# Quarter products in the up-projection, sums of squares ahead of TensorE, and later gate projections in a hybrid decoder layer

## The chip, the core and the metric

The kernel runs on one core of one Trainium2 chip. The metric is device time in microseconds (us). TensorE multiplies matrices into PSUM, VectorE, ScalarE and GpSimd work elementwise, and DMA queues move data; the kernel issues its DMAs from the SP queue. The executions shown for the kernel before took 1553.11, 1553.45 and 1550.46 us, with a median of 1553.11 us.

## What is computed

One inference step of one decoder layer, for 16 learned meta tokens and 1024 prompt tokens and, beside them, 8 samples of 4 tokens each. That makes 1072 columns of 1024 features. Everything is float32.

```
h = rms_norm(x, norm_mix); proj = h @ w_in             # 1024 -> 4104
o_ret = retention(rq, rk, rv) ...                       # 4 heads, chunked, with states
o_gdn = gated delta rule(conv(qkv), gates gb, ga) ...   # 4 heads, chunked, with states
x = x + concat(o_ret * silu(rg), o_gdn * silu(gg)) @ w_out
u = causal width-3 depthwise conv(rms_norm(x, norm_ffn) @ w_up)   # 1024 -> 2 * 2816
gate, val = split(u)
x = x + (silu(gate) * val) @ w_down
y = rms_norm(x, norm_final)
```

The states of retention, of the delta rule and of both convolutions are returned too.

## The kernel before

Activations lie with features on the partitions and tokens along the columns. `ob` holds x and later results; `hh` and `hl` hold the normalised activations as a rounded high part and the remainder. Each weight tile (128 outputs by 1024 inputs) is loaded in two DMAs into `raw`, split into `whi` (a ScalarE cast) and `wlo` (a VectorE subtraction), and a product is three matmuls for each of 8 slices of 128 inputs: high by high, high by low, low by high (`mm3`, line 574). The moving operand is a block of columns.

The order of all instructions is worked out by a planner in the kernel (`Recorder`, lines 206 to 466). Operations are recorded first. Then each engine takes, at the planner's assumed time, the ready operation of the lowest class (`cls`) and the earliest record, given a free buffer in the ring of each tile it needs; buffers of one ring are given out in the order of recording within a stream. Projection matmuls are class 2, most chains class 1, evacuations and weight loads class 0. The result is one fixed order for each engine. All instructions are issued at line 466, so they are told apart by tile names.

The stages:

- Head (lines 634 to 724). x arrives in three blocks of columns, `BLK_A`. For each, `x_sums` squares the eight slices (ScalarE, partly VectorE) and sums each over the features by one-column matmuls against `ones_t`, three for each slice; `x_stats` makes the inverse roots and spreads them over the partitions; `x_split` writes `hh` and `hl`. Eight gate columns (`wg`) are projected block by block in the same loop with `g1` and `g2`, 16 matmuls for each block.
- Mixing (lines 745 to 1228). Gate values first, then jobs in a written order: four delta-rule heads ("g"), four retention heads ("r"), and gate tiles ("w"). Projections in ring `mm` (3 PSUM banks) fill the gaps of the chains, which use ring `mx` (5 banks).
- Output projection (lines 1247 to 1353). Blocks 0 and 1 of `BLK_B` (384, 384 and 290 columns) first, then block 2 with all weights loaded again; the normalisation of finished blocks runs beside it.
- Feed-forward (lines 1355 to 1500). 22 pairs of up tiles, one for the gate and one for the value. `up` (line 1357) makes three blocks of 384, 386 and 292 columns with 24 matmuls each; the convolution is one ScalarE and two VectorE operations for each block; then silu, the product (GpSimd) and a split into `r15`. After each two pairs, a group, `down` (line 1481) adds 8 output tiles by 3 blocks, 6 matmuls each, into `ob`. The down weights are split on GpSimd.
- Tail: in the last group the down tiles go block by block (`final`, line 1396), with the squares, the inverse roots and the scaled output of each block behind it.

Of the kernel before, what the change touches and what calls it, by code (L numbers as in the profile page):

```python
# [45 lines left out]
BLK_B = ((0, 384), (384, 768), (768, 1058))  # L46
# [433 lines left out]
def build(tc, I, O, debug=None):  # L480
# [33 lines left out]
    ring(const, "whi", 2, KD * P, F32R)  # L514
    ring(const, "wlo", 2, KD * P, F32R)
# [48 lines left out]
    def load_w(src, lo_eng=None, tags=("raw", "raw")):  # L564
        with cls(0):
            hi = buf("whi", [P, KD, P])
            lo = buf("wlo", [P, KD, P])
            for a, tag in zip((0, 4), tags):
                raw = buf(tag, [P, 4, P])
                dma(out=raw, in_=src[:, a:a + 4, :])  # L570
                split(hi[:, a:a + 4, :], lo[:, a:a + 4, :], raw, lo_eng or V)
        return hi, lo
# [19 lines left out]
    def fetch(t):  # L592
        if t is not None and t not in wq:
            wq[t] = load_w(w_in[t])
# [13 lines left out]
    def gate_proj(slot, nxt, tag):  # L608
# [7 lines left out]
        proj(gate_tile(slot), nxt, evac)  # L616

    with tc.tile_pool(name="mp", bufs=1) as mp:
# [17 lines left out]
        rsx, ssx, tsx, msx, mhx = (buf("c8", [P, 9]) for _ in range(5))  # L636
        G.memset(ssx, 1.0)
# [8 lines left out]
        def x_sums(i):  # L646
            b0, b1 = BLK_A[i]
            n = b1 - b0
            pss = [bank() for _ in range(3)]
            for k in range(KD):  # L650
                sq = buf(("gkd", "gvb", "gy32")[k % 3], [P, 384])
# [5 lines left out]
                for q in range(3):  # L657
                    c0, c1 = chunk_cols(3 * i + q)
                    T.matmul(pss[q][0:c1 - c0, 0:1], sq[:, c0 - b0:c1 - b0], ones_t[:, 0:1], start=k == 0, stop=k == KD - 1)
            for q in range(3):  # L660
                c = 3 * i + q
                c0, c1 = chunk_cols(c)
                V.tensor_copy(ssx[0:c1 - c0, c:c + 1], pss[q][0:c1 - c0, 0:1])

        def x_stats(i):
            b0, b1 = BLK_A[i]
            cs = slice(3 * i, 3 * i + 3)
            ss, ms, mh, rs_, t_ = (b[:, cs] for b in (ssx, msx, mhx, rsx, tsx))
            V.tensor_scalar(out=ms, in0=ss, scalar1=1.0 / D, scalar2=EPS, op0=ALU.mult, op1=ALU.add)
# [27 lines left out]
        g1 = buf("whi", [P, KD, P])  # L697
        g2 = buf("wlo", [P, KD, P])
        graw = buf("c40", [P, KD, 8])
        dma(out=graw, in_=I["wg"])  # L700
        fetch(16)
        x_cols(1, 4)
        x_cols(2, 4)
        last = R.ops[-1]
        for g in (g1, g2):
# [5 lines left out]
        for i, (b0, b1) in enumerate(BLK_A):  # L711
            x_split(i, spread)
            if i < 2:
                spread, last_sqrt = x_stats(i + 1)
# [849 lines left out]
```

## Time and profile before

| | us |
|---|---|
| median of the runs shown | 1553.11 |
| the profiled execution | 1549.05 |
| its span, first to last instruction | 1547.2 |
| TensorE busy | 1505.8 |
| VectorE busy | 976.2 |
| ScalarE busy | 582.3 |
| GpSimd busy | 301.3 |

The profile shows one execution. Busy times on TensorE overlap, because matmuls are pipelined and a row's own length reaches past the next row's start; what a matmul costs is read from the distance of two starts. "Idle before" names the work that released an engine. Times of stretches count from the span's start.

### The profile page before, as it was taken

The page shows a single profiled execution, that of the slowest core. Times are in us where ns is not written, and L with a number is a line of the kernel's source. Part 1 is how long each engine was busy: PE and PEld are TensorE (multiplying, and loading weights), DVE is VectorE, ACT ScalarE, POOL GpSimd, SP SyncE. Part 2 cuts the span into 40 slices and gives each one's busy share as a digit, 9 for nine tenths or more (in the row PEclk, how much of TensorE's full clock was granted, in tenths as well). Part 3 has the DMA queues.
Part 4 walks back from the last instruction along what each step waited for, and adds up shares of the span by engine and source line. Part 5 has one row for each costly group of instructions (what it writes and reads, how often), then busy time and mean ns, then how long its engine had stood idle before and what let it go on. Part 6 is the DMA issues. An engine that isn't in the chain of part 4 may idle for free.

```text
span 1547.2 us, 25949 instructions
## 1 busy us (share of the span) xinstructions
PE 1505.8 (97%) x9875; PEld 1453.0 (94%) x9875; DVE 976.2 (63%) x2411; ACT 582.3 (38%) x1553; POOL 301.3 (19%) x365
## 2 busy tenths in 40 slices
PE   7999999999999999999999999999999999999994
PEld 7898988999899899999999999999999999999994
DVE  4787787787768856647854545545554545555547
ACT  4553453455346335424532232324132231324123
POOL 1221202202120221501320212113020212112022
PEclk9999999999999999999999999999999999999997
DMA  5121202111120211523120110202021111202103
GB/s 189 30 72 29 84 20 70 43 59 60 41 81 28 63 33 53 183 83 96 49 76 28 56 60 25 75 23 70 20 64 28 56 52 33 68 29 70 42 1 114
DMA packets 63689, 91.06 MB, mean 59 GB/s; under 512 B 13060, under 2 KB 31948, under 8 KB 63436
## 3 DMA queue, kind: packets, MB, share of 16 engines
q1 hardware_dynamic: 63564, 89.40, 18.3%
q8 instruction: 78, 1.28, 0.4%
q14 instruction: 47, 0.39, 0.1%
HBM read 79.71 MB, written 9.66 MB: 58 GB/s over the span
## 4 chain that ended last, share of the span: by engine, by line
PE 90%; DVE 6%; DMA 1%; issue 1%; ACT 1%; POOL 0%; SPq 0%; DVEq 0%; ACTq 0%; POOLq 0%
PE mm L466 61%; PE mx L466 29%; DVE wlo L466 1%; DVE ob L466 1%; DMA ob<-in_xt 1%; DVE sw L466 1%; DVE c L466 1%; DMA gbq<-scr_rows 0%; ACT f2k L466 0%; SPq L466 0%; POOL f2k L466 0%; DVE f2k L466 0%; DVE t2k L466 0%; DVE gvb L466 0%; DVE hl L466 0%
## 5 line engine op out<-in xcount | busy, mean ns | idle before, releaser
L466 PE MATMUL mm<-hh,whi 128*128 128x384 f32 (+5 forms) x1952 | 643.5, 330 | 1.7 <-ACT hh L466 1.0
L466 PE MATMUL mm<-hh,wlo 128*128 128x384 f32 (+5 forms) x1952 | 644.5, 330 | 0.0
L466 PE MATMUL mm<-hl,whi 128*128 128x384 f32 (+5 forms) x1952 | 642.3, 329 | 0.4 <-POOL hl L466 0.3
L466 PEld LDWEIGHTS mm<-hh,whi 128*128 128x128 f32 x1952 | 368.8, 189 | 4.8 <-issue 1.5
L466 PEld LDWEIGHTS mm<-hl,whi 128*128 128x128 f32 x1952 | 369.2, 189 | 3.2 <-issue 0.9
L466 PEld LDWEIGHTS mm<-hh,wlo 128*128 128x128 f32 x1952 | 368.6, 189 | 1.7 <-issue 0.5
L466 DVE SCALAR_TENSOR_TENSOR f2k<-mm,wc,f2k 128x352 f32<-128x352 f32 (+2 forms) x264 | 150.9, 572 | 160.7 <-ACT f2k L466 80.0
L466 PE MATMUL mx<-r,dhl 128*128 128x384 f32 (+1 forms) x1440 | 232.5, 321 | 0.0
L466 PEld LDWEIGHTS mx<-r,dhl 128*128 128x128 f32 x1440 | 231.9, 188 | 0.0
L466 ACT ACTIVATE f2k<-mm,wc 128x352 f32<-128x352 f32 (+1 forms) x132 | 72.0, 545 | 306.7 <-PE mm L466 306.7
L466 DVE TENSOR_TENSOR ob<-mx,ob 128x384 f32<-128x384 f32 (+1 forms) x240 | 123.3, 524 | 100.7 <-PE mx L466 98.4
L466 DVE TENSOR_TENSOR wlo<-raw,whi 128x512 fp32r<-128x512 f32 x170 | 137.2, 820 | 33.1 <-ACT whi L466 32.6
L466 ACT CAST whi<-raw 128x512 fp32r<-128x512 f32 x170 | 103.9, 620 | 43.5 <-PE mm L466 36.0
L466 POOL TENSOR_TENSOR f2k<-f2k,f2k 128x384 f32<-128x384 f32 (+1 forms) x75 | 76.6, 1022 | 173.4 <-DVE f2k L466 160.1
L466 POOL TENSOR_SCALAR f2k<-su,wc 128x32 f32<-128x32 f32 x44 | 13.5, 306 | 443.9 <-ACT su L466 443.9
L466 POOL TENSOR_TENSOR ob<-ob,sw 128x384 f32<-128x384 f32 (+1 forms) x39 | 41.9, 1074 | 210.5 <-DVE sw L466 145.4
L466 ACT ACTIVATE f2k<-f2k 128x384 f32<-128x384 f32 (+1 forms) x66 | 32.9, 499 | 115.8 <-DVE f2k L466 115.8
L466 DVE TENSOR_TENSOR r<-f2k,r 128x384 fp32r<-128x384 f32 (+1 forms) x66 | 34.8, 528 | 60.3 <-ACT r L466 60.2
L466 ACT CAST r<-f2k 128x384 fp32r<-128x384 f32 (+1 forms) x66 | 32.4, 490 | 93.7 <-POOL f2k L466 93.7
L466 POOL TENSOR_TENSOR dhl<-f2k,dhl 128x512 fp32r<-128x512 f32 x44 | 55.6, 1298 | 11.8 <-ACT dhl L466 11.8
L466 DVE SCALAR_TENSOR_TENSOR ob<-mm,wc,ob 128x384 f32<-128x384 f32 (+3 forms) x90 | 51.3, 570 | 1.7 <-ACT ob L466 1.2
L466 DVE TENSOR_TENSOR ob<-mm,ob 128x384 f32<-128x384 f32 (+1 forms) x48 | 25.0, 522 | 38.4 <-PE mm L466 38.1
(282 smaller groups left out, 1830.7 us busy)
## 6 DMA issues: line engine op xcount, KB each, us to landing
raw<-in_w_up SPq DMA_DIRECT2D x88, 256.0 KB, 2.7
raw<-in_w_in SPq DMA_DIRECT2D x64, 256.0 KB, 2.9
f2k<-in_w_down SPq DMA_DIRECT2D x44, 256.0 KB, 4.5
raw<-in_w_out SPq DMA_DIRECT2D x18, 256.0 KB, 2.8
gbq<-scr_rows SPq DMA_DIRECT2D x16, 256.0 KB, 4.2
out<-sst SPq DMA_DIRECT2D x8, 512.0 KB, 2.6
wr<-in_w_out SPq DMA_DIRECT2D x14, 256.0 KB, 3.0
ob<-in_xt SPq DMA_DIRECT2D x4, 768.0 KB, 8.3
```

Of the source, the lines that this page charges most:

```text
L466: f(*a, **k)
```

## The change

Head: the squares of eight slices are added elementwise into two accumulators, and only these are summed over the features, by six one-column matmuls a block. The gate projection and its chain move into a function `gates`, recorded behind the second delta-rule tile, and use ring `mm`. The low parts of three early weight tiles (16, 20, 24) are made on GpSimd. Weight buffers are rings of half tiles.

Output projection: blocks are 508, 276 and 274 columns wide, with the two narrow ones first and the wide one last; three weight tiles are kept for both rounds. While the wide block is projected, the narrow ones are normalised and the operand sums of the quarter products are formed (`norm_others`); the wide one is normalised inside the first pair (`norm_first`).

Feed-forward: for the two narrow blocks, a pair of up tiles (two row blocks), the two halves of the inputs and the two blocks of columns make a 2 by 2 product of quarters, computed with seven products instead of eight, from sums of weights (on GpSimd) and sums of activations, and additions of results (on VectorE). The wide block is projected as before. The down-projection takes two banks of `mx` as ring `dn`, and its weights come in quarters.

```diff
-BLK_B = ((0, 384), (384, 768), (768, 1058))
+BLK_O = ((0, 508), (508, 784), (784, 1058))
+BLK_B = ((0, 510), (510, 784), (784, 1058))
+WS = 276
+HB = (508, 782)
...
-    ring(const, "whi", 2, KD * P, F32R)
-    ring(const, "wlo", 2, KD * P, F32R)
+    ring(const, "whi", 4, KD * P // 2, F32R)
+    ring(const, "wlo", 4, KD * P // 2, F32R)
...
-            wq[t] = load_w(w_in[t])
+            wq[t] = load_w(w_in[t], G if t in (16, 20, 24) else None)
...
-            pss = [bank() for _ in range(3)]
+            acc = []
             for k in range(KD):
...
-                for q in range(3):
-                    c0, c1 = chunk_cols(3 * i + q)
-                    T.matmul(pss[q][0:c1 - c0, 0:1], sq[:, c0 - b0:c1 - b0], ones_t[:, 0:1], start=k == 0, stop=k == KD - 1)
+                if k < 2:
+                    acc.append(sq)
+                else:
+                    (V if k % 2 else G).tensor_tensor(out=acc[k % 2][:, 0:n], in0=acc[k % 2][:, 0:n], in1=sq[:, 0:n], op=ALU.add)
+            pss = bank()
...
+                for j in range(2):
+                    op = T.matmul(pss[0:c1 - c0, q:q + 1], acc[j][:, c0 - b0:c1 - b0], ones_t[:, 0:1], start=j == 0, stop=j == 1)
...
-        dma(out=graw, in_=I["wg"])
         fetch(16)
         x_cols(1, 4)
+        dma(out=graw, in_=I["wg"])
...
+                if h == 0 and i == 1:
+                    R.stream = 3
+                    gates()
+                    R.stream = 0
...
+        for tag, n, e, dt in (("al", 4, 512, F32R), ("as", 8, 274, F32R), ("dhl", 4, 512, F32R), ("f2k", 5, 512, F32), ("ds", 8, WS, F32),
+                              ("rawd", 1, 512, F32), ("su", 6, NB * 6, F32), ("uo", 2, 72, F32), ("c3", 8, 4, F32)):
...
+        R.rings["dn"] = Ring(mx.bufs)
+        mx.free.sort(key=lambda f: f[1])
+        R.rings["dn"].free = [mx.free.pop() for _ in range(2)]
+        more("raw", 2, F32)
+        more("whi", 2, F32R)
+        more("wlo", 2, F32R)
...
-        gate_proj(3, None, "f2k")
+        gate_proj(3, None, "f2k", BLK_A[::-1])
...
+        def prod(out, a, x, first=True, last=True):
+            with cls(2):
+                for k in range(4):
+                    xh, xl = x(k)
+                    T.matmul(out, a[0][:, k, :], xh, start=first and k == 0, stop=False)
+                    T.matmul(out, a[0][:, k, :], xl, start=False, stop=False)
+                    T.matmul(out, a[1][:, k, :], xh, start=False, stop=last and k == 3)
...
+                r11, r12, r21, r22 = (load_half(w_up[f], a) for f in fs for a in (0, 4))
+                a11, a12, a21, a22 = (unit(r) for r in (r11, r12, r21, r22))
+                G.tensor_tensor(out=r22, in0=r21, in1=r22, op=ALU.add)
+                G.tensor_tensor(out=r21, in0=r11, in1=r21, op=ALU.subtract)
+                G.tensor_tensor(out=r11, in0=r22, in1=r11, op=ALU.subtract)
+                G.tensor_tensor(out=r12, in0=r12, in1=r11, op=ALU.subtract)
+                s2, s1 = (unit(r) for r in (r11, r22))
+                s3, s4 = (unit(r, None, ("al", "al") if late else ("whi", "wlo")) for r in (r21, r12))
...
+            x = one(a11, B11)
+            m1 = buf("ds", [P, WS])
+            with cls(0):
+                S.copy(m1, x)
+            g1 = []
+            if late is None:
+                first_block(lambda: g1.append(second()))
+            else:
+                g1.append(second())
+            v = one(a22, T4, "mx")
+            u2 = buf("ds", [P, WS])
+            add(u2, one(s2, T2), m1)
+            z = one(s1, T1)
+            u3 = buf("ds", [P, WS])
+            add(u3, one(s3, T3), u2)
+            add(u2, z, u2)
+            v1_ = conv(add(v, v, u3), NF + p, 1, uo, None)
+            v2_ = conv(add(z, z, u3), NF + p, 2, uo, None)
+            z = one(s4, B22)
+            g2_ = conv(add(z, z, u2), p, 2, uo, None)
+            if late is not None:
+                late()
+                first_block()
...
+            R.stream = 1
             if not tail:
...
+                wd = [down_weights(mq) for mq in range(2)]
+                for m in range(4):
+                    down(wd[m // 2], m, 0)
+                for m in range(4):
+                    for t in (1, 2):
+                        down(wd[m // 2], m, t)
+                for mq in (2, 3):
+                    wd = down_weights(mq)
+                    for m in (2 * mq, 2 * mq + 1):
                         for t in range(3):
-                            down(wd, m, t, "mx")
+                            down(wd, m, t)
...
```

Here `first_block` projects the wide block for both tiles of the pair (24 matmuls each in ring `mx`), `second` is the product of `a12` with `B21`, added to `m1`, and `conv` is the convolution. The lines above leave out the new bodies of `norm_others`, `norm_first`, `gates` and `down_weights`, whose work the text above tells.

## Rows read from the trace of the kernel before

**Rows 1.** The page's part 1: busy time of each engine, share of the span.
```profile
PE 1505.8 (97%) x9875; PEld 1453.0 (94%) x9875; DVE 976.2 (63%) x2411; ACT 582.3 (38%) x1553; POOL 301.3 (19%) x365
```
**Rows 2.** The chain that ended last, one feed-forward group: start, us, what.
```profile
1101.53 46.86 PE mm L466 x288
1148.40 23.09 PE mx L466 x144
```
**Rows 3.** Busy times by stretch: length, PE, PEld, DVE, ACT, POOL, granted clock, DMA.
```profile
62.00:630.00 568.00, 557.40 (x4081) 512.54 (x4080) 433.55 (x1302) 269.46 (x816) 110.31 (x138) 1.00 0.17 53
720.00:770.00 50.00, 47.67 (x313) 45.76 (x312) 45.40 (x107) 26.23 (x59) 15.51 (x18) 1.00 0.21 66
837.00:907.00 70.00, 70.00 (x434) 70.00 (x434) 36.61 (x70) 20.05 (x49) 12.32 (x14) 1.00 0.15 47
1510.20:1530.00 19.80, 12.98 (x73) 12.17 (x72) 14.67 (x35) 11.89 (x29) 9.60 (x11) 0.74 0.07 23
```
**Rows 4.** Timeline of TensorE in the feed-forward: start, us, engine, instruction.
```profile
894.52 0.30 PE L466 MATMUL mm<-hh,whi 128*128 128x292 f32 x1
...
897.78 0.34 PE L466 MATMUL mm<-hh,whi 128*128 128x384 f32 x1
...
901.97 0.34 PE L466 MATMUL mm<-hh,whi 128*128 128x386 f32 x1
```
**Rows 5.** Instruction groups, 837 to 907 us: count, busy, mean ns, idle before.
```profile
L466 DVE TENSOR_TENSOR wlo<-raw,whi 128x512 fp32r<-128x512 f32 x8 | 6.9, 861 | 2.8 <-ACT whi L466 2.8
L466 POOL TENSOR_TENSOR dhl<-f2k,dhl 128x512 fp32r<-128x512 f32 x4 | 5.1, 1300 | 1.1 <-ACT dhl L466 1.1
L466 ACT CAST whi<-raw 128x512 fp32r<-128x512 f32 x8 | 5.0, 622 | 1.9 <-PE mm L466 1.9
...
L466 DVE TENSOR_TENSOR ob<-mx,ob 128x290 f32<-128x290 f32 x8 | 3.7, 459 | 1.5 <-PE mx L466 1.4
```
**Rows 6.** Timeline of TensorE in the head, 0 to 62 us.
```profile
4.54 1.23 PE L466 MATMUL mx<-ones_t,gkd 128*48 128x1 f32 x6 [4.54 <-ACT gkd L466]
...
12.82 1.26 PE L466 MATMUL mx<-ones_t,gvb 128*48 128x1 f32 x6
...
23.78 0.60 PE L466 MATMUL mm<-hh,whi 128*128 128x304 f32 x1
...
31.83 0.46 PE L466 MATMUL mm<-hh,wlo 128*128 128x304 f32 x1
32.08 0.46 PE L466 MATMUL mm<-hh,whi 128*128 128x304 f32 x1
...
33.62 0.30 PE L466 MATMUL mm<-hl,whi 128*128 128x304 f32 x1
33.77 0.30 PE L466 MATMUL mm<-hh,wlo 128*128 128x304 f32 x1
...
46.18 0.53 PE L466 MATMUL mm<-hh,whi 128*128 128x388 f32 x1
```
**Rows 7.** Timeline of VectorE in the head, 0 to 62 us.
```profile
20.32 1.42 DVE L466 SCALAR_TENSOR_TENSOR t2k<-ob,wc,mx 128x304 f32<-128x304 f32 x3 [2.14 <-PE mx L466]
```
**Rows 8.** The chain that ended last, 740 to 770 us.
```profile
752.96 0.75 PE mx L466 x6
...
762.10 0.81 POOL hl L466
```
**Rows 9.** Timeline of all engines in the tail, 1503 to 1548 us.
```profile
1510.68 6.72 ACT L466 ACTIVATE f2k<-ob 128x384 f32<-128x384 f32 x16
...
1512.05 8.24 POOL L466 TENSOR_TENSOR f2k<-f2k,f2k 128x290 f32<-128x290 f32 x7 [19.18 <-DVE f2k L466]
...
1521.20 4.79 PE L466 MATMUL mm<-r,dhl 128*128 128x290 f32 x22 [0.82 <-DVE r L466]
...
1538.75 5.13 DVE L466 SCALAR_TENSOR_TENSOR ob<-ob,wc,mx 128x384 f32<-128x384 f32 x11
```
**Rows 10.** One tile's view, wlo, 780 to 1500 us: durations ns min/median/max, starts.
```profile
L466 DVE TENSOR_TENSOR wlo<-raw,whi x80: 691/693/1368, 781.2 to 1470.4; 128x512 fp32r<-128x512 f32 x80
```

More of the change, by code (lines that the diff above doesn't have):

```diff
@@ L1225, in build @@
         wq[None] = wo[0]
-        keep = [v.vt for t in wq.values() for v in t]
+        keep = [v.vt for t in wq.values() for x in t for v in x.parts]
         for v in keep:
@@ new lines, in sums, with up_pair, one, add @@
+        def sums(i):
+            return lambda k: (th[:, i, k, :], tl[:, i, k, :])
+        B11, B21 = (cols(k, slice(HB[0], HB[0] + WS)) for k in (0, 4))
+        B22, T1 = cols(4, slice(HB[1], HB[1] + WS)), cols(0, slice(BLK_O[2][0], BLK_O[2][0] + WS))
+        T2, T3, T4 = (sums(i) for i in range(3))
+        def up_pair(p, uo, late=None):
+            fs = (p, NF + p)
+            sus = []
+            with cls(0):
+                for f in fs:
+                    su = buf("su", [P, NB, 6])
+                    dma(out=su, in_=I["sff"][:, f * NB * 6:(f + 1) * NB * 6].rearrange("p (b t) -> p b t", b=NB))
+                    sus.append(su)
+                r11, r12, r21, r22 = (load_half(w_up[f], a) for f in fs for a in (0, 4))
[6 more added lines that the diff above has]
+                s3, s4 = (unit(r, None, ("al", "al") if late else ("whi", "wlo")) for r in (r21, r12))
+            def one(a, b, tag="mm"):
+                out = bank(tag)[:, 0:WS]
+                prod(out, a, b)
+                return out
+            def add(out, a, b):
+                with cls(0):
+                    V.tensor_tensor(out=out, in0=a, in1=b, op=ALU.add)
+                return out
+            whole = []
+            def first_block(then=None):
+                for f, (ka, kb) in zip(fs, ((a11, a12), (a21, a22))):
+                    out = bank()[:, 0:510]
+                    prod(out, ka, cols(0, CL), last=False)
+                    prod(out, kb, cols(4, CL), first=False)
+                    whole.append(conv(out, f, 0, uo, sus[f // NF]))
+                    if then is not None and f == p:
+                        then()
+            def second():
+                x2 = one(a12, B21)
+                return conv(add(x2, x2, m1), p, 1, uo, None)
+            x = one(a11, B11)
+            m1 = buf("ds", [P, WS])
+            with cls(0):
+                S.copy(m1, x)
[18 more added lines that the diff above has]
+                first_block()
+            return (whole[0], g1[0], g2_), (whole[1], v1_, v2_)
@@ L1430, in final @@
                 rb = bank()
[L1431 removed]
+                dg = buf("f2k", [P, 4, P])
                 for i, (a, b) in enumerate(cuts):
```

445 lines of the change are left out of this document (238 added, 207 removed).

## Prediction

> **What bounds the kernel now.** I read the page's busy times first. TensorE is busy 97% of the span, VectorE 63%, ScalarE 38%, GpSimd 19% [rows 1]: the matmuls are the candidate. Busy time on TensorE is not proof, so I read the chain of waits next. In the feed-forward it is nothing but matmuls: 46.86 us for 288 up-projection matmuls, 23.09 us for 144 down-projection ones [rows 2]. That pair of rows repeats, one pair of lines for each of the 11 groups (the last is drawn out by the tail). One group takes 69.95 us and TensorE idles in none of it, while VectorE is busy 36.61 of 70 us, ScalarE 20.05, GpSimd 12.32 [rows 3]. So half of the execution (770 us) is bound by the number and width of matmuls alone, and only fewer columns can shorten it.
>
> The stretch views show three places of another kind. In the mixing stretch (62 to 630 us) VectorE is 76% busy and TensorE idles 10.6 of 568 us, 1.9% [rows 3]. At the junction of output projection and feed-forward (720 to 770 us) VectorE is 91% busy, and TensorE idles 2.3 of 50 us [rows 3]. In the head and in the tail TensorE waits for chains; both are priced below.
>
> **The feed-forward.** For each pair of 128-row up tiles the old code runs 2 x 3 blocks x 24 matmuls of 384, 386 and 292 columns. The new one runs 2 x 24 matmuls of 510 columns and seven products of 12 matmuls of 276 columns, where eight would be needed in the plain way. What does a matmul of each width cost? I take start-to-start times, since TensorE is pipelined and a row's own length is not its price. 24 starts of 292 columns, 894.52 to 897.78 us, give 0.1358 us each; the next 24 of 384 columns, to 901.97, give 0.1746 [rows 4]. The line through the two is 0.00042 us per column. It gives 0.129 us for 276 columns and 0.228 for 510; neither width occurs in the trace. Bounds: 276 columns lie between 0.128 (in proportion to 292) and 0.136 (no faster than 292, if the weight load sets a floor there); 510 lie between 0.226 and 0.232 (in proportion to 384). I take the line, because 276 is only 16 columns from a measured width.
>
> A group holds two pairs. Its up part becomes 96 x 0.228 + 168 x 0.129 = 21.9 + 21.7 = 43.6 us, against 46.86: 3.3 us less, 36 us over 11 groups. The bounds: 96 x 0.226 + 168 x 0.128 = 43.2 (40 us gained) and 96 x 0.232 + 168 x 0.136 = 45.1 (19 us gained). The down part keeps its 144 matmuls, now of 510, 274 and 274 columns: 48 x (0.228 + 2 x 0.128) = 23.2 us instead of 23.09, 1 us lost in all. The output projection changes its widths in the same way, 192 x (0.227 + 0.129 + 0.128) us, under 1 us of difference.
>
> The Trainium skill speaks of this sum: "TensorE: Matmul & The Clock Gate", section "Back-to-back issue gap", puts an isolated full-clock matmul at its columns over 2.4 GHz plus 2.5 ns. That would be 162.5 ns for 384 columns, where rows 4 have 174.6. By it the up part would go from 43.2 us to 40.4 and the gain would be 31 us: the same sign, a little less. The rows decide.
>
> **What the seven products cost the other engines.** For each pair, eight half-size weight units are split into high and low parts instead of four: four more ScalarE casts of 0.622 us and four more VectorE subtractions of 0.861 us [rows 5]. Four 512-column sums of weights go to GpSimd, priced by its 512-column subtraction of 1.300 us. Seven additions from PSUM go to VectorE, by the 290-column addition of 0.459 us [rows 5]. For each group of two pairs that is, on VectorE, 8 x 0.861 + 14 x 0.459 = 13.3 us more, 36.6 to 49.9; ScalarE goes from 20.1 to about 26.8 (two copies of some 0.4 us with it), GpSimd from 12.3 to 22.7. All three still fit under the 66.8 us of TensorE. But VectorE would be 75% busy, and TensorE has less room to wait: two of the five mx banks become a ring of their own for the down tiles ("dn"), a product must wait for its bank, and a bank is held until VectorE has added and convolved. Queued behind a late addition on VectorE are the convolution taps, then the gate product, then the split that the down matmuls read. These waits do not occur in the trace of before; I bound them by two stretches. At 53% of VectorE TensorE waits for nothing (lower end 0). At 76% it idles 1.9%, which is 1.25 us of a group. At 91%, at the junction, it idles 4.7%, 3.1 us of a group (upper end, 34 us in all). The load of 75% is nearest to the mixing stretch, so I take 1.25 us x 11 = 14 us. The added DMA issues (44 small loads of conv states in place of one) go to the SP queue, which issues in a fraction of a microsecond; they stand ahead of weights that are asked for a pair in advance, so I price them at nothing; uncovered, the weights would come late once a pair and this would be part of the 14 us.
>
> **Head.** TensorE starts the one-column sums of block 0 at 4.54 us and the last run until about 14 us; VectorE begins to normalise block 0 only at 20.32 us [rows 6, 7]. TensorE then alternates projections with the one-column sums of blocks 1 and 2, and the 24 matmuls of the first projection block, begun at 23.78, are followed by the next block only at 46.18 [rows 6]. Moreover it runs at the 1.2 GHz level there: 304 columns start 0.25 us apart at 31.8 and 0.15 apart at 33.6 [rows 6]. The change removes 54 of 72 one-column matmuls and adds 18 elementwise additions on VectorE and GpSimd. Block 0's sums then end some 4 us earlier, because six matmuls follow the last square instead of a queue of 24 fed since 4.54. The gates' 48 matmuls are moved, not removed; behind two tiles they run at full clock. Their chain of small operations on ScalarE, VectorE and GpSimd must then be done before the first recurrent job, with one more tile as cover (24 x 0.15 + 48 x 0.175 = 12 us); if that falls short, other projections fill in. Their weight load moves behind block 1's input on the SP queue and is needed only two tiles later: nothing. What is late next is the split of blocks 1 and 2 on VectorE, which also does the convolutions there. Lower end of the gain: 3 us, the earlier first split less one addition of about 1 us. Upper end: 13 us, the 54 matmuls at about 0.2 us (11 us) and the first tile at full speed. I take 8. It passes to the end, since TensorE has projections left to fill with when mixing ends.
>
> **Junction.** The last output tiles now belong to the widest block, and its normalisation is hidden behind pair 0's seven products, 84 x 0.129 = 10.8 us. Before, the chain from the sums at 752.96 us to the last awaited split, ending at 762.91 [rows 8], is 10 us for 290 columns. With 508 columns each of its long operations is 1.6 times as long, so some 14 to 17 us; the 5.5 us of the first wide product use the split rows one by one. I expect the same loss as before, 0, within 4 us either way.
>
> **Tail.** ScalarE's squares (6.72 us from 1510.68) and GpSimd's additions (8.24 us from 1512.05) stand ahead of the last block's gate product and split, so its down matmuls run in earnest only from 1521.20 [rows 9]. Between 1510.2 and 1530 TensorE is busy 12.98 of 19.8 us, at a mean granted clock of 0.74 [rows 3]. In the new order the wide block's 48 down matmuls (10.9 us) and the middle block's (6.2 us) lie behind the last product: 17 us of work cover an 11 us chain. Then the end is VectorE's: its last scalings run to 1543.9 [rows 9], and their columns stay the same. Gain from 0 (VectorE bound all through) to 12 (the idle 6.8 us and the slow clock); I take 8.
>
> **The sum** is made against the profiled execution, 1549.05 us with a span of 1547.2: -36 + 2 (other widths) + 14 (waits) - 8 - 8 = -36. The median of the runs shown, 1553.11, is 4 us above that execution, so the forecast on the scale of the runs is 1517 us.
>
> **Rivals.** (a) The planner hides all waits: 0 instead of 14, head and tail at 11 each: -36 + 2 - 22 = -56, 1497 us. For it: the old feed-forward has not one wait. Against it: VectorE had 47% free there. (b) The waits are those of the junction, 34 us, and tail and head give 4 each: -36 + 2 + 34 - 8 = -8, 1545 us. For it: two down banks, and additions, taps and weight splits falling together in a pair's second half.
> (c) Slower: GpSimd's added work blocks VectorE until VectorE is the bound. In the feed-forward the weight subtraction takes 0.691 to 1.368 us with a median of 0.693 [rows 10]: some take twice as long. If the added GpSimd operations doubled all 16 weight subtractions and the 6 of the activations, VectorE would need 49.9 + 16 x (1.368 - 0.861) + 6 x 0.5 = 61 us a group; adding a doubling of the 24 down additions that fall to it (by 0.5) gives 73 us. From 71.4 us a group (69.95 plus the head's and the tail's 16 us over 11) the kernel is slower; at 73, 11 x 3 - 16 = +18, 1571 us. Against it: GpSimd has work for only a third of a group, and the down additions read one operand from PSUM.
> The Trainium skill has the rule behind this rival: "SBUF — State Buffer", section "Who interferes with whom", says that a VectorE instruction with two SBUF inputs contends with a GpSimd one that reads SBUF, and that the loser waits for the whole instruction. The maximum in rows 10 agrees; that PSUM additions should be free of it speaks against (c).
> (d) The seven products do not shorten TensorE because 276 columns meet a floor: at 0.136 us the feed-forward gains 19 instead of 36; it is in the bounds, 1534 us.
>
> **Chances.** Forecast, 1502 to 1535 us with the floor of (d) at its upper end: 0.50. (a): 0.22. (b): 0.14. Within 0.2%, about what a measurement of this kernel can tell from no change (1550 to 1556): 0.04. (c): 0.10. So faster 0.86, same 0.04, slower 0.10. The range takes in (a) and most of (b): 1493 to 1545.
>
> **What would show it.** Steps: 84 products a pair about 0.129 us apart and 48 about 0.228; the chain's up pieces near 43.6 us a group; VectorE near 50 us a group. Wrong if: idle time of TensorE before "mm" or "dn" matmuls released by VectorE exceeds 3 us a group; VectorE is over 90% busy there; the first split is not before 17 us; TensorE still idles over 5 us after the last product.

## The result, and the profile after

The changed kernel takes 1531.89 us (median of 4 runs, 1531.76 to 1533.05) beside 1552.3 us of the kernel before on the same chip: a ratio of 0.9871, interval 0.9854 to 0.9888. That is 20 us less; the profiled spans, 1547.2 and 1530.1 us, give 17.1. The forecast was 36 us less. The sign holds and the time lies in the range; half of the gain is missing, so the question is where it went. Line 466 of before is line 469 here.

Busy times after, part 1 of the page (before: rows 1), and busy times by stretch (columns as in rows 3):
```profile
PE 1471.4 (96%) x9513; PEld 1329.2 (87%) x9513; DVE 1127.7 (74%) x2661; ACT 643.9 (42%) x1684; POOL 459.6 (30%) x502
...
62.00:630.00 568.00, 561.36 (x4082) 511.48 (x4081) 428.48 (x1300) 268.72 (x811) 110.31 (x140) 1.00 0.17 52
720.00:770.00 50.00, 42.80 (x215) 37.16 (x215) 42.07 (x78) 23.82 (x54) 28.15 (x25) 0.93 0.17 53
837.00:904.40 67.40, 67.30 (x409) 60.60 (x408) 49.20 (x92) 25.14 (x58) 23.20 (x22) 1.00 0.16 50
645.00:657.00 12.00, 7.39 (x37) 6.73 (x37) 10.04 (x20) 8.78 (x32) 12.00 (x22) 0.72 0.60 178
```
The feed-forward group (third stretch) is close to the forecast: 67.4 us instead of 69.95, with VectorE busy 49.2, ScalarE 25.1 and GpSimd 23.2 us (forecast: 66.8 and 1.25 of waits, 49.9, 26.8 and 22.7). The junction (second) is not: TensorE idles 7.2 of 50 us, where it was 2.3 [rows 3], and the mean granted clock is 0.93. The last stretch, the start of the output projection, is new: TensorE is busy 7.4 of 12 us at a clock of 0.72. In the kernel before, the same stretch is full:
```profile
645.00:657.00 12.00, 12.00 (x71) 12.00 (x70) 10.58 (x14) 6.33 (x15) 7.94 (x8) 1.00 0.98 313
```

The starts of TensorE at the borders of the parts (first matmul of the output projection, first of the feed-forward, last of the last product), in the kernel before and in the changed one:
```profile
645.02 0.52 PE L466 MATMUL mm<-r,whi 128*128 128x384 f32 x2
...
741.44 0.34 PE L466 MATMUL mm<-hh,whi 128*128 128x384 f32 x1
...
1509.91 0.30 PE L466 MATMUL mm<-hh,wlo 128*128 128x292 f32 x1
```
```profile
643.22 0.36 PE L469 MATMUL mm<-th,whi 128*128 128x276 f32 x1 [0.49 <-POOL tl L469]
...
748.56 0.29 PE L469 MATMUL mm<-hh,whi 128*128 128x276 f32 x1
...
1484.50 0.29 PE L469 MATMUL mm<-hh,wlo 128*128 128x276 f32 x1
```
From these starts the difference of the two profiled executions splits up like this (us):

| part | forecast | measured |
|---|---|---|
| up to the first matmul of the output projection (645.02, now 643.22) | -8 | -1.8 |
| output projection (96.4, now 105.3) | under +1 | +8.9 |
| first pair of the feed-forward (junction) | 0 | +10.3 |
| 11 groups (69.95, now 67.41 each) | -36 + 1 + 14 = -21 | -27.9 |
| tail (time behind the last product less its down matmuls: 31.6, now 24.9) | -8 | -6.7 |
| sum | -36 | -17.2 (17.1 by the rounded spans) |

The junction's line is what is left of the stretch from output projection to last product (768.6, now 736.1) after the groups' 27.9 us and 14.9 us of down matmuls that have moved behind the last product. There are 36 of 510 and 96 of 274 columns there now, 20.5 us at 0.232 and 0.127 us each; there were 42 of 290 columns, 5.6 us at 0.133. The measured column compares one execution of each kernel. In the eight profiles below and above that have the changed head, the last projection matmul starts between 640.4 and 642.7 us, so the first line is known to about 2 us.

TensorE in one group after, and the same matmul eight groups later (timeline; answers rows 4):
```profile
848.82 0.29 PE L469 MATMUL mm<-hh,whi 128*128 128x276 f32 x1
...
851.87 0.63 PE L469 MATMUL mx<-al,dhl 128*128 128x510 f32 x2
...
856.34 0.39 PE L469 MATMUL mx<-hh,whix 128*128 128x510 f32 x1
...
861.91 0.29 PE L469 MATMUL mm<-hh,whix 128*128 128x276 f32 x1
...
1388.09 0.29 PE L469 MATMUL mm<-hh,whi 128*128 128x276 f32 x1
```
24 starts of 276 columns, 848.82 to 851.87, are 0.127 us each; 24 of 510, 856.34 to 861.91, are 0.232. The forecast had 0.129 and 0.228. (1388.09 - 848.82) / 8 = 67.41 us a group.

TensorE's waits at the two places that cost 19 us (timeline; in brackets the idle time and what ended it):
```profile
650.10 0.60 PE L469 MATMUL mm<-th,whi 128*128 128x276 f32 x1 [3.60 <-ACT th L469]
651.68 0.60 PE L469 MATMUL mm<-tl,whi 128*128 128x276 f32 x1 [0.98 <-DVE tl L469]
...
753.10 0.29 PE L469 MATMUL mx<-th,whix 128*128 128x276 f32 x1
759.35 1.85 PE L469 MATMUL mx<-ones_t,f2k 128*128 128x1 f32 x8 [5.96 <-DVE f2k L469]
```
At 753 us one matmul of a product is followed by the wide block's sums of squares, and TensorE's queue stands for 6 us. What it waits for, on ScalarE, GpSimd and VectorE:
```profile
755.76 0.62 ACT L469 CAST al<-raw 128x512 fp32r<-128x512 f32 x1 [3.76 <-POOL raw L469]
756.29 0.62 ACT L469 ACTIVATE f2k<-ob 128x508 f32<-128x508 f32 x1
...
753.26 1.25 POOL L469 TENSOR_TENSOR f2k<-f2k,f2k 128x508 f32<-128x508 f32 x1
754.47 1.26 POOL L469 TENSOR_TENSOR raw<-rawx,raw 128x512 f32<-128x512 f32 x1
...
757.15 1.59 POOL L469 TENSOR_TENSOR rawx<-rawx,rawx 128x512 f32<-128x512 f32 x1
...
756.41 1.21 DVE L469 TENSOR_TENSOR al<-raw,al 128x512 fp32r<-128x512 f32 x1 [3.87 <-ACT al L469]
757.54 1.75 DVE L469 TENSOR_TENSOR f2k<-f2k,f2k 128x508 f32<-128x508 f32 x1
```
The last square (ScalarE, 756.29) is queued behind a cast that waits for GpSimd's sums of weights, and the last sum of squares (VectorE, 757.54) behind the subtraction that follows that cast. And it takes 1.75 us for 508 columns.

The head (timelines of VectorE, GpSimd, TensorE):
```profile
17.07 0.97 DVE L469 SCALAR_TENSOR_TENSOR t2k<-ob,wc,mx 128x304 f32<-128x304 f32 x2 [0.89 <-PE mx L469]
...
32.20 3.44 DVE L469 SCALAR_TENSOR_TENSOR ob<-sc,wc,ob 128x32 f32<-128x32 f32 x3
...
32.13 1.30 POOL L469 TENSOR_TENSOR wlo<-raw,whi 128x512 fp32r<-128x512 f32 x1 [0.21 <-ACT whi L469]
33.39 0.99 POOL L469 TENSOR_TENSOR gkd<-gkd,gy 128x384 f32<-128x384 f32 x1
34.34 1.26 POOL L469 TENSOR_TENSOR wlo<-raw,whi 128x512 fp32r<-128x512 f32 x1
...
36.77 0.44 PE L469 MATMUL mm<-hh,whi 128*128 128x388 f32 x1 [3.66 <-ACT hh L469]
```
The first split comes at 17.07 instead of 20.32 us [rows 7], 3.25 us earlier, near the 3 us forecast. But then three VectorE operations of 32 columns take 3.44 us, and TensorE waits 3.66 us for the split queued behind them.

### The profile page after: what moved, and what is told of

Its sections match the earlier page's. It is cut to its first block, busy times and chain, and to the rows that moved or that the text cites. A ratio compares the mean times of both kernels' runs of the same rounds, so it can differ in the third digit from the quotient of the medians.

```text
span 1530.1 us, 25981 instructions
## 1 busy us (share of the span) xinstructions
PE 1471.4 (96%) x9513; PEld 1329.2 (87%) x9513; DVE 1127.7 (74%) x2661; ACT 643.9 (42%) x1684; POOL 459.6 (30%) x502
## 4 chain that ended last, share of the span: by engine, by line
PE 84%; DVE 11%; ACT 2%; issue 2%; DMA 1%; POOL 0%; SPq 0%; DVEq 0%; ACTq 0%; POOLq 0%
PE mx L469 45%; PE mm L469 39%; DVE ob L469 2%; DVE wlo L469 2%; DVE ds L469 1%; DVE c L469 1%; DVE hl L469 1%; DVE f2k L469 1%; DVE sw L469 1%; DVE t2k L469 0%; DVE wlox L469 0%; DMA ob<-in_xt 0%; DVE gvb L469 0%; ACT jk L469 0%; ACT hh L469 0%
## 5 line engine op out<-in xcount | busy, mean ns | idle before, releaser
L469 PE MATMUL mm<-hh,whi 128*128 128x384 f32 (+5 forms) x1084 | 357.7, 330 | 6.7 <-ACT hh L469 5.5
L469 PE MATMUL mm<-hl,whi 128*128 128x384 f32 (+5 forms) x1084 | 357.5, 330 | 2.9 <-DVE hl L469 2.9
L469 PE MATMUL mm<-hh,wlo 128*128 128x384 f32 (+5 forms) x1084 | 357.4, 330 | 0.0
L469 PEld LDWEIGHTS mm<-hh,whi 128*128 128x128 f32 x1084 | 206.6, 191 | 13.9 <-ACT hh L469 6.5
L469 PEld LDWEIGHTS mm<-hl,whi 128*128 128x128 f32 x1084 | 206.6, 191 | 9.9 <-DVE hl L469 4.2
L469 PEld LDWEIGHTS mm<-hh,wlo 128*128 128x128 f32 x1084 | 206.7, 191 | 4.3 <-issue 1.3
L469 DVE TENSOR_TENSOR ob<-mx,ob 128x274 f32<-128x274 f32 (+1 forms) x264 | 136.0, 522 | 99.5 <-PE mx L469 96.4
L469 PEld LDWEIGHTS mx<-as,dhl 128*128 128x128 f32 x1008 | 143.2, 190 | 16.7 <-DVE ob L469 8.5
L469 PE MATMUL mx<-as,dhl 128*128 128x274 f32 x1008 | 153.3, 293 | 1.4 <-DVE ob L469 0.4
L469 PE MATMUL mx<-al,dhl 128*128 128x510 f32 x504 | 134.2, 394 | 3.1 <-ACT al L469 2.0
```

Source lines behind the costliest of these rows:

```text
L469: f(*a, **k)
```

## Experiments

The changed kernel was timed once more beside the first three (1533.5 us; ratio 0.9881, 0.9866 to 0.9895, span 1531.7). Differences below are from that run.

**What do the seven products give?** Eight plain products in the same new order:
```diff
-            v = one(a22, T4, "mx")
...
-            g2_ = conv(add(z, z, u2), p, 2, uo, None)
+            v1_ = conv(two(a21, a22, B11, B21, "mx"), NF + p, 1, uo, None)
+            v2_ = conv(two(a21, a22, B12, B22), NF + p, 2, uo, None)
+            g2_ = conv(two(a11, a12, B12, B22), p, 2, uo, None)
```


> The changed kernel with the plain eight quarter products (96 matmuls of 276 columns a pair instead of 84), with no sums of weights, no sums of inputs and no additions from PSUM, in the same order of blocks and with the same head and tail. Theory 1 (the feed-forward is bound by the columns that TensorE streams, 0.127 us a matmul of 276, and the elementwise work of the seven products hides): a group of the feed-forward takes 24 x 0.127 = 3.0 us more than the changed kernel's 67.4, so 70.4, that is 33 us over 11 groups; less up to 5 us at the junction, where the sums of inputs and weights are gone: 28 to 34 us slower than the changed kernel, ratio to the kernel before 1.005 to 1.010. Rival (the seven products pay a good part of their saving back in waits, as the forecast had it with 1.25 us a group): a group takes 1.5 to 2.3 us more than 67.4 and the whole is 12 to 24 us slower than the changed kernel.

1545.67 us, ratio 0.997 (0.9959 to 0.9982), span 12.1 us longer. The whole is in the rival's range, the group between the two. TensorE's timeline of this run, one matmul eight groups apart, and its stretches:
```profile
832.82 0.29 PE L469 MATMUL mx<-hh,whi 128*128 128x276 f32 x1
...
1391.54 0.29 PE L469 MATMUL mx<-hh,whi 128*128 128x276 f32 x1
...
720.00:770.00 50.00, 50.00 (x270) 43.41 (x269) 37.04 (x77) 25.58 (x52) 19.46 (x17) 1.00 0.24 71
```
A group takes 69.84 us, 2.43 more than 67.41; the columns alone would make 24 x 0.127 = 3.05. So the seven products give back 0.6 us a group. Eleven groups would make 27 us, but the whole is only 12 longer: outside the steady groups the plain products save some 15 us. Split as in the table above, 9 of these lie at the junction, 3 in the tail and the rest ahead of the feed-forward, where profiles of the same work differ by 1 to 2 us. At the junction TensorE is busy 50.00 of 50 us at the full clock. The junction's loss thus belongs to the seven products, whose first pair needs sums of inputs and of weights all at once, and not to the new order of the blocks.

**Is the junction's wait one of order?** Wide tiles' evacuation first, combined weights of pair 0 behind it:
```diff
+            with cls(-1 if w > 2 * KD - 4 else R.cls):
...
-                (G if KD < w < 2 * KD - 1 else V).tensor_tensor(out=acc[:, 0:n], in0=acc[:, 0:n], in1=sq[:, 0:n], op=ALU.add)
+                    done[0] = (G if KD < w < 2 * KD - 2 else V).tensor_tensor(out=acc[:, 0:n], in0=acc[:, 0:n], in1=sq[:, 0:n], op=ALU.add)
...
+                    for op in R.ops[n0:]:
+                        if op.eng == "S":
+                            op.preds.add(done[0])
```


> The changed kernel with another order at the junction: additions, squares and sums of the last three wide output tiles go ahead of weight work on every engine, the last two sums of squares are on VectorE instead of GpSimd, and the casts of pair 0's four combined weight units stand behind the last sum. Theory 1 (TensorE's 6.25 us wait at 753 us is one of order: the last sum of squares is queued on GpSimd and VectorE behind sums and splits of weights): the wait falls under 2.5 us and the whole is 4 to 8 us shorter than the changed kernel. Rival (VectorE has too much to do there, as it was 91% busy at the junction before): the wait only moves to the wide block's splits or to the combined weights, and the whole is within 1.5 us of the changed kernel.

1525.84 us, ratio 0.9838 (0.9825 to 0.9852): 7.7 us shorter by the medians, 6.7 by the ratios, theory 1. From the first feed-forward matmul to the last product it takes 731.5 us instead of 736.1. The wait of TensorE falls from 6.0 to 3.55 us, not under 2.5. What is left of it shows on VectorE and GpSimd in this run:
```profile
754.86 1.72 DVE L469 TENSOR_TENSOR f2k<-f2k,f2k 128x508 f32<-128x508 f32 x1 [0.69 <-ACT f2k L469]
...
754.78 1.26 POOL L469 TENSOR_TENSOR rawx<-raw,rawx 128x512 f32<-128x512 f32 x1
756.12 1.60 POOL L469 TENSOR_TENSOR rawx<-rawx,rawx 128x512 f32<-128x512 f32 x1
```
The last sum of squares still takes 1.72 us while GpSimd adds weights. With pair 0's sums of weights on VectorE (the run of both places, below) the same operation takes
```profile
753.40 0.69 DVE L469 TENSOR_TENSOR f2k<-f2k,f2k 128x508 f32<-128x508 f32 x1 [0.69 <-ACT f2k L469]
```

**The start of the output projection.**
```diff
             def down_weights(mq, tags=("dhl", "dhl")):
-                with cls(0):
+                with cls(0 if gp else 1):
```


> The changed kernel with the first group's down-projection weights asked for and split in program order instead of as early as possible, so that their ScalarE casts and GpSimd subtractions no longer stand among the evacuations of the last gate tile. Theory 1 (the two waits of 3.9 and 1.6 us at 646 to 652 us, and the clock of 0.5 that follows them, come from these casts and subtractions): waits together under 2.5 us and the whole 3 to 8 us shorter. Rival (the chain tanh, product, gate product, cast, subtraction is that long by itself behind the last gate block): the waits stay above 4 us and the whole is within 1.5 us of the changed kernel.

1529.69 us, ratio 0.9861 (0.9848 to 0.9875): 3 to 4 us shorter, with an interval that overlaps the changed kernel's. The time alone does not settle it; the first wait does, which is 3.6 us in every profile that leaves this place as it was and 2.22 here. With the second, 1.58, the waits are 3.8 us together: between the two theories. The casts and subtractions of the down weights were part of the cause. The rest, as far as this run's rows show it, is the last gate tile's own chain and a weight subtraction of 1.52 us on VectorE in the middle of it.

**Does VectorE's share make the waits?** The four sums of weights of each pair on VectorE:
```diff
-                G.tensor_tensor(out=r22, in0=r21, in1=r22, op=ALU.add)
+                V.tensor_tensor(out=r22, in0=r21, in1=r22, op=ALU.add)
...
```


> The changed kernel with the four sums of weights of each pair on VectorE instead of GpSimd: eight more VectorE operations a group of about 0.7 us each (5.5 us, from 50 to some 54 of 67.4 us net of shorter subtractions), GpSimd 10 us a group less. Theory 1 (TensorE's waits in the feed-forward come from order at single places and not from VectorE's share, so that a share of 80% adds no wait): a group stays within 0.3 us of 67.4; at the junction, where GpSimd's sums overlap VectorE's sums of squares, which then took 1.7 instead of 0.7 us, 1 to 3 us are gained: the whole 0 to 4 us shorter. Rival (waits grow with VectorE's share, as read between the rows of 53, 76 and 91%): 0.7 us more a group, 8 us longer.

1523.64 us, ratio 0.9827 (0.9813 to 0.984): 8.4 us shorter by the ratios. The rival falls, since the sign is the other one. Theory 1 holds in that a higher share of VectorE adds no wait, but it had the whole at most 4 us shorter. First the changed kernel's stretch and what TensorE's weight loads wait for in it (line waited for: us, times, longest) with one weight subtraction (durations in ns, min/median/max), then this kernel's; it has no such wait:
```profile
840.00:1430.00 590.00, 589.20 (x3575) 531.04 (x3574) 435.09 (x814) 224.93 (x520) 205.63 (x196) 1.00 0.16 49
...
PEld mx L469 <- DVE ob L469: 6.6, 17, 0.4
...
L469 DVE TENSOR_TENSOR wlo<-raw,whi x55: 678/1284/1820, 782.9 to 1466.8; 128x512 fp32r<-128x512 f32 x55
```
```profile
840.00:1430.00 590.00, 590.00 (x3607) 536.38 (x3606) 450.72 (x889) 225.79 (x520) 113.01 (x124) 1.00 0.16 50
...
L469 DVE TENSOR_TENSOR wlo<-raw,whi x55: 673/692/1380, 783.4 to 1459.2; 128x512 fp32r<-128x512 f32 x55
```
VectorE's share rises from 73.7% to 76.4%, and the waits vanish. Beside GpSimd's sums the median of these weight subtractions was 1.284 us, without them 0.692; the other 55 of that tile, which read `rawx`, have 0.68 in both kernels. The same matmul eight groups apart (848.10 and 1382.54 us) gives 66.81 us a group: 0.60 less than 67.41, and 3.03 less than with eight products, which is what the columns alone make. (The 0.83 us in a later expectation compared starts that were not the same matmul.)

**The head as a whole**, undone in the changed kernel:
```diff
-            pss = bank()
...
+                for q in range(3):
+                    T.matmul(pss[q][0:c1 - c0, 0:1], sq[:, c0 - b0:c1 - b0], ones_t[:, 0:1], start=k == 0, stop=k == KD - 1)
...
-                    gates()
...
-            wq[t] = load_w(w_in[t], G if t in (16, 20, 24) else None)
+            wq[t] = load_w(w_in[t])
```


> The changed kernel with the old head: 72 one-column sums of squares fed square by square, the gates' 48 matmuls back among the blocks of the input, weight subtractions of tiles 16, 20, 24 back on VectorE; feed-forward, output projection and tail as changed. Theory 1 (the new head begins to split 3 us earlier, but VectorE, busy 13.9 of the 14 us from 32 to 46 us, then sets the pace, so that nearly nothing reaches the end): 0 to 4 us slower than the changed kernel, gate tile 3 done within 4 us of the changed kernel's 643.2 us. Rival (the head gave the 8 us of the forecast, and something in the mixing stretch took 6 of them back): 6 to 10 us slower, with the loss visible at the end of mixing; or, if the new head's order itself is what harmed mixing, 2 to 6 us faster.

1535.7 us, ratio 0.9907 (0.9893 to 0.992): 2 to 4 us longer. The last projection matmul, in the changed kernel timed again, in this one, and in the run without GpSimd's weight subtractions that follows below:
```profile
641.38 0.30 PE L469 MATMUL mm<-hh,wlo 128*128 128x304 f32 x1
```
```profile
643.63 0.30 PE L469 MATMUL mm<-hh,wlo 128*128 128x304 f32 x1
```
```profile
635.49 0.30 PE L469 MATMUL mm<-hh,wlo 128*128 128x304 f32 x1
```
The new head is worth about 2 us, as theory 1 has it, but its reason still had to be tried.

**The gates' place.**
```diff
+            tiles = [op for op in R.ops if op.eng == "T"][-1]
...
+                        op.preds.add(tiles)
```


> The changed kernel with the gates' 46 matmuls kept back until the second tile's last matmul, so that they run behind two tiles at the full clock, as the forecast took them to; in the changed kernel they ran among the blocks of the first tile from 28 us on, partly at half clock. Theory 1 (in the head VectorE sets the pace, and the gates only fill time that TensorE idles anyway): between 1 us shorter and 4 us longer than the changed kernel, since the same waits of TensorE before 50 us are then empty and the gates' 7 us come behind them. Rival (the missing 6 us of the head's forecast are the gates' place): 3 to 6 us shorter.

1531.38 us, ratio 0.9876 (0.986 to 0.9892): no difference, theory 1. Where the gates stand doesn't matter in this kernel.

**Is VectorE full in the head?** A kernel that leaves out two of the three taps in two tiles:
```diff
-                        for j in (2, 1, 0):
+                        for j in (2,) if t in (16, 20) else (2, 1, 0):
```


> The changed kernel without two of the three convolution taps on VectorE in the first two tiles projected (left out: taps 1 and 0 of tiles 16 and 20, 12 operations of about 0.5 us, 6 us of VectorE between 30 and 60 us), nothing else. Theory 1 (between the first split and about 60 us VectorE sets the pace of the head, 13.9 of 14 us busy from 32 to 46): TensorE's waits before 60 us, 10.9 us in the changed kernel, fall by 3 us or more, and the last gate tile is done 3 to 6 us earlier. Rival (the head's lead is lost to TensorE's own work, the gates' matmuls and the half clock, not to VectorE): the waits stay within 2 us and the last gate tile is done within 2 us of the changed kernel.

1529.58 us, ratio 0.9856 (0.984 to 0.9873). TensorE's starts more than 0.5 us apart between 10 and 62 us sum to 13.3 us, against 14.0; the longest is 3.97 us in both; the last projection matmul comes 1.7 us earlier, at 639.7, which is 0.6 us below the lowest of the profiles with the whole head. Theory 1, on which I had rested the head, falls: taking work off VectorE does not shorten the wait. The numbers are the rival's, but not its cause, since the gates' matmuls made no difference above. The interval overlaps the changed kernel's, so the 3 to 4 us by the ratio may be chance in part.

**Does GpSimd block it?**
```diff
-            wq[t] = load_w(w_in[t], G if t in (16, 20, 24) else None)
+            wq[t] = load_w(w_in[t])
```


> The changed kernel with the weight subtractions of input tiles 16, 20 and 24 back on VectorE, as in the kernel before; the rest of the head as changed. In the changed kernel three VectorE operations of 32 columns took 3.45 us at 30.9 us, in the same stretch in which GpSimd ran two of these weight subtractions (1.3 us each) and an addition back to back, and TensorE then waited 3.97 us for the first split of block 1. Theory 1 (VectorE's operations with two inputs wait out GpSimd's whole instructions, so GpSimd's work blocks the head at that place): the three short operations fall under 1.5 us, TensorE's wait of 3.97 us under 2 us, and the last gate tile is done 2 to 5 us earlier. Rival (VectorE is full there, and six more subtractions of 0.7 us cost it what the blocking cost): the waits before 60 us stay within 1.5 us in all, and the last gate tile comes within 2 us of the changed kernel.

1526.03 us, ratio 0.9848 (0.9835 to 0.9861), 5.1 us shorter by the ratios and 7.5 by the medians; the last projection matmul at 635.5 instead of 641.4 us: theory 1, with more than it asked for. The wait of 3.97 us is gone: between 25 and 46 us no two starts of TensorE lie more than 0.8 us apart. The short operations (durations in ns, min/median/max), in the kernel before, in the changed one, and in this one:
```profile
L466 DVE SCALAR_TENSOR_TENSOR ob<-sc,wc,ob x3: 239/239/241, 48.7 to 51.0; 128x32 f32<-128x32 f32 x3
```
```profile
L469 DVE SCALAR_TENSOR_TENSOR ob<-sc,wc,ob x3: 915/1182/1275, 32.2 to 34.5; 128x32 f32<-128x32 f32 x3
```
```profile
L469 DVE SCALAR_TENSOR_TENSOR ob<-sc,wc,ob x6: 238/240/1012, 30.5 to 57.4; 128x32 f32<-128x32 f32 x6
```
The one of 1.012 us starts at 41.36 us, beside a GpSimd subtraction of 1.03 us that starts at 41.29. And the head's stretch, in the changed kernel timed again and in this one:
```profile
14.00:62.00 48.00, 39.13 (x190) 33.85 (x191) 39.18 (x81) 25.01 (x60) 24.11 (x24) 0.93 0.25 84
```
```profile
14.00:62.00 48.00, 43.45 (x221) 37.02 (x222) 43.49 (x95) 28.00 (x69) 20.87 (x20) 0.96 0.27 91
```
VectorE is busier by 4.3 us, and TensorE too.

**Put together.** First the two places of order, with pair 0's sums of weights on VectorE and the last gate tile's evacuation first (added to the edits of both places, with the down weights in class 2 instead of 1):
```diff
-            with cls(0):
+            with cls(-1 if slot == 3 else 0):
...
-                G.tensor_tensor(out=ob[:, slot, b0:b1], in0=ob[:, slot, b0:b1], in1=th[:, 0:n], op=ALU.mult)
+                (V if slot == 3 else G).tensor_tensor(out=ob[:, slot, b0:b1], in0=ob[:, slot, b0:b1], in1=th[:, 0:n], op=ALU.mult)
...
+                    with cls(-1 if t == 1 and k == 3 else R.cls):
...
-                G.tensor_tensor(out=r22, in0=r21, in1=r22, op=ALU.add)
+                (V if late else G).tensor_tensor(out=r22, in0=r21, in1=r22, op=ALU.add)
...
```


> The changed kernel with both places mended: the junction's order as in the run of its own that gave 7.7 us (sums of squares ahead of weight work), with pair 0's four sums of weights on VectorE besides; and at the start of the output projection the first group's down weights behind the out-projection's tiles, the last gate tile's evacuation and the split of its slice first on every engine, its gate product on VectorE instead of GpSimd. Theory 1 (the two places are independent, and both are order): 7.7 + 3.8 = 11.5 us, and 2 to 4 us more from the two extras, so 11 to 15 us shorter than the changed kernel, 1517 to 1522 us, near the time forecast. Rival (they share the same slack of VectorE, and what is gained at the first place is waited for at the second): no more than 8 us shorter.

1525.19 us, ratio 0.9837 (0.9823 to 0.985): 6.8 us shorter by the ratios, 8.3 by the medians, the rival's number. The output projection was 2.5 to 4.7 us shorter (102.8 us, against 105.3 and 107.5 in the two runs of the changed kernel), but three sums of weights (749.98 to 752.03 us) now stood ahead of the last wide tile's addition on VectorE, and the sums of squares came 4.0 us late. With those sums placed behind it, and all sums of weights on VectorE:
```diff
...
+                    for op, after in zip(R.ops[-3:], (done[1], done[0], done[0])):
+                        op.preds.add(after)
...
```


> The changed kernel with the three things that helped put together: all sums of weights on VectorE (8.4 us by ratios alone); the sums of squares of the last wide tiles ahead of weight work (7.7 us alone), with pair 0's second sum of weights behind the last addition to the residual and its third and fourth behind the last sum of squares; and the start of the output projection as in the run of both places, which shortened that projection by 3 to 5 us. Theory 1 (three separate places: GpSimd's sums slow VectorE in every group, 0.83 us x 11 = 9 us; order at the junction, 4 to 5 us that the first item doesn't hold already; order at the start of the output projection, 3 us): 15 to 18 us shorter than the changed kernel, ratio to the kernel before 0.976 to 0.979, some 1515 us. Rival (the runs of the first two shared one cause, GpSimd's sums beside VectorE's sums of squares at the junction, and the feed-forward itself gave less): 9 to 12 us shorter, ratio 0.980 to 0.983.

1515.6 us, ratio 0.9762 (0.9747 to 0.9776): 18 us shorter, theory 1. And with the head's three weight tiles back on VectorE, by the edit shown above:

> The kernel with the three mended things (all sums of weights on VectorE, the junction's order, the start of the output projection), which gave 1515.6 us and a ratio of 0.976, with the weight subtractions of tiles 16, 20 and 24 back on VectorE as well. Theory 1 (the head's blocking is a place of its own): 2 to 5 us shorter again, ratio 0.973 to 0.975. Rival (VectorE is full in the head): within 1.5 us of 1515.6, ratio 0.975 to 0.977.

1508.32 us, ratio 0.9734 (0.9721 to 0.9747): 4 us more by the ratios, 7 by the medians; theory 1. This version beats both kernels, by 41 us and by some 23. Its page's busy times, and its waits at the two places (timeline):
```profile
PE 1458.9 (97%) x9513; PEld 1322.2 (88%) x9513; DVE 1144.0 (76%) x2759; ACT 646.0 (43%) x1684; POOL 337.9 (22%) x404
...
640.59 0.39 PE L469 MATMUL mm<-th,whi 128*128 128x276 f32 x1 [2.13 <-ACT th L469]
...
743.79 1.05 PE L469 MATMUL mx<-ones_t,f2k 128*128 128x1 f32 x8 [1.93 <-DVE f2k L469]
```

## Why the prediction was right in sign and too large

The time lies in the stated range, but that range is 52 us wide. Output projection and junction lost 19 us that were priced at under 1, and the head gave 6 less than forecast. That the feed-forward gave 7 more was not foreseen either; without it the time would lie near the upper end of the range.

- **Columns.** Right. 0.127 and 0.232 us for 0.129 and 0.228; 43.6 us of up part forecast, 96 x 0.232 + 168 x 0.127 = 43.6 measured; a group without waits is 66.81 us, against 66.8 forecast. That the sum is hit so closely is in part luck: 0.127 lies just under the lower bound and 0.232 at the upper, and the two errors, 0.3 and 0.4 us a group, cancel. The floor of rival (d), 0.136, is not there. By the rule of the Trainium skill that stood beside this sum, "TensorE: Matmul & The Clock Gate", section "Back-to-back issue gap", the two widths would take 0.1175 and 0.215 us; the rows are 8% longer, and the measurement decides.
- **Waits in the feed-forward.** Forecast 1.25 us a group, measured 0.60 (67.41 - 66.81). Rival (a) had 0 here, so the truth lies between the two. The size was off by half, and the step that gave it, reading the wait from VectorE's share, failed: at 76.4% TensorE waits for nothing when GpSimd does not make the sums of weights. That was rival (c), whose mechanism is there and whose price was not: it makes single operations late, it does not make VectorE the bound.
- **Output projection.** Forecast under 1 us, measured 8.9. The step priced widths alone. Not priced: what stands on ScalarE and GpSimd when the last gate tile is evacuated. The tile's slice is the last of the first output tile's eight, the down weights have a buffer of their own and were split right there, and TensorE, which was full there before, waits 3.60 and 0.98 us. Behind these waits the granted clock is at its half level, so that 276 columns start 0.23 us apart from 652 to 655 us and 0.127 again from 656 (mean clock 0.72 from 645 to 657). Narrow blocks first also leave less ahead of that slice: 21 matmuls are 2.7 us at 0.127, where 384 columns at 0.1746 would make 3.7. No run tested this by itself.
- **Junction.** Forecast 0 within 4, measured 10.3. The step compared a longer chain with a longer cover and took the chain to start on time. It starts late: the first pair's sums of weights, priced only as steady work, stand ahead of the last squares. Order alone gave back 4.6 us of it between the first feed-forward matmul and the last product (6.7 to 7.7 of the whole run); a sum of squares that took 1.7 instead of 0.7 us beside GpSimd is the rest that could be seen.
- **Head.** Forecast 8, measured 1.8. The reasoning on sums and splits held. With the three weight tiles' subtractions left on VectorE, the last projection matmul comes at 635.5 us, 8.1 before the 643.6 of the old head. The nearness to 8 is luck, since 8 was the middle of 3 to 13. The step that failed is a line of the diff that I did not price: it moves six subtractions of 1.3 us to GpSimd, where the first splits of block 1 then wait for them.
- **Tail.** Forecast 8, measured 6.7. Right in size.
- **The signs of being wrong.** Two of the four came: the first split starts at 17.07 us, not before 17, and TensorE idles 7.5 us in all between the last product and its last matmul (13.4 before), more than the 5 named. The other two did not: VectorE is busy 73% of a group, and TensorE idles 0.1 us in one.

The rule that I weighed under rival (c), from the Trainium skill, "SBUF — State Buffer", section "Who interferes with whom", is that a VectorE instruction with two SBUF inputs and a GpSimd one that reads SBUF contend for a port pair that is an exclusive lock. The runs agree: 0.24 us became 0.92 to 1.28 beside GpSimd operations of 0.99 to 1.30. Additions with one operand in PSUM show no such delay, which settles what was weighed against (c). The down additions of the wide block, first in the changed kernel timed again, then with the sums of weights on VectorE (groups from 840 to 1430 us: count, busy, mean ns, idle before):
```profile
L469 DVE TENSOR_TENSOR ob<-mx,ob 128x510 f32<-128x510 f32 x68 | 45.7, 683 | 30.3 <-PE mx L469 30.3
```
```profile
L469 DVE TENSOR_TENSOR ob<-mx,ob 128x510 f32<-128x510 f32 x68 | 46.5, 683 | 30.1 <-PE mx L469 30.1
```
I had used this rule for a sum over a group, where its price is small; it decides at places where TensorE's next operand is in VectorE's queue.

Open: what decides how long the half clock behind a wait lasts. At the start of the output projection the last two versions have the same waits (2.1 and 0.9 us), but from 638 to 657 us a mean clock of 0.91 in the first and 1.00 in the second. Open too are the 3 to 4 us of the run without taps, of which the head shows 1.7 at most.

## What to carry to other kernels

Price every instruction that a change moves to GpSimd at the places where VectorE's queue feeds TensorE, not by the engine's spare time: GpSimd had two thirds of its time free, and its sums of weights cost 6.6 us in the feed-forward and its weight subtractions some 4 to 7 us in the head. A saving that repeats needs a set-up once, here sums of inputs and weights for the first pair; look for it at the seam, and put what the next stage waits for ahead of it on every queue. An engine that is 99% busy in a stretch may be waiting inside its instructions: compare the duration of one instruction with the same form elsewhere before calling the engine full.

## What the runs showed of the hardware

Three VectorE operations on 32 columns took 0.92 to 1.28 us each beside GpSimd additions and subtractions, 0.24 without them; a 512-column subtraction 1.284 us (median) and 0.692; a 508-column addition 1.72 and 0.69. A 510-column addition with one operand in PSUM took 0.683 us in both cases. Busy time counts this waiting as work, so VectorE's share was higher for the same instructions. Moving eight additions a group from GpSimd to VectorE raised VectorE's busy time only by 15.6 of 590 us, though 75 more instructions, 72 of them these sums at about 0.7 us each, ran in it.
